# mLSTM v and o of two heads at a time by seven half-size products, attention output parked in DRAM, and another order of the heads' steps

## The chip, the cores and the metric

One core of a Trainium2 chip. Its engines work side by side, each through its own queue in order: PE (TensorE, matrix products, and transposes by an identity), ACT (ScalarE), DVE (VectorE), POOL (GpSimd, which here computes reciprocal square roots and issues DMAs, among them the ones that add to what lies in memory), SP (SyncE, which issues the plain weight loads). The metric is device time of one launch in microseconds, lower is better.

## The reference, cut to what matters

One layer of a decoder trunk: 512 tokens of width 1024, float32. A half-step feed-forward block, a mixer, a second half-step block, with RMS norms between. The mixer has a dilated attention and an mLSTM side by side:

```python
proj = h @ w_in     # attention q,k,v | mLSTM q,k (conv), v, o | mLSTM i,f | branch gates
...                 # attention: 3 groups of 4 heads of 128 channels, groups combined to att (512 x 512)
qk = jax.nn.silu(causal_depthwise_conv(qk_m, conv_w, conv_b))
q_m, k_m = jnp.split(qk, 2, axis=-1)              # mLSTM: 4 heads of 256 channels
hm = mlstm_chunkwise(q_m, k_m, v_m, ig, lf)       # heads are independent of each other
hm = hm * lax.rsqrt(jnp.mean(hm * hm, axis=-1, keepdims=True) + RMS_EPS)
hm = hm * head_g
ml = jax.nn.sigmoid(o_m) * hm
merged = jax.nn.sigmoid(g_a) * (att @ w_att_branch) + jax.nn.sigmoid(g_m) * (ml @ w_mlstm_branch)
return merged @ w_out
```

The change concerns `v_m` and `o_m`: the 512 x 1024 matrix h times 512 columns for each head (256 of v, 256 of o).

## The kernel before

Every float32 factor is held as two fp32r parts, high (`wh`, `hTh`) and low (`wl`, `hTl`); a product is three matmuls (high x high, low x high, high x low). `load_w` lets SP load a block of weights (512 KB) into `wf`, ACT cast it to `wh`, and DVE subtract to `wl`; `split` does the last two for a block that is in memory already.

Some products are done by seven half-size products instead of eight (Strassen's scheme in Winograd's form): tokens, inner dimension and columns are halved, and sums and differences of the quarters are multiplied. The token side's sums are made once (`token_sums`: parts 4, 5, 6, 7 in `x7`; the quarters themselves are 1, 2, 3) and partly parked in DRAM (`kept`), from where `reload6` and `reload4` fetch them. The weight side's sums are made by POOL's DMAs that add one block of DRAM to a tile: `v12_sums` and `v12_seven` for the attention's v of groups 1 and 2 (tiles `sum_x` and `sum_z`, products `pwa`, `pwb`, `pwc`). In `unit` DVE makes them, for the branch gates of the mLSTM (`gm1` to `gm7`).

Order of the mixer: q, k, scores, softmax and values of four attention head slots (`scores`, `turn`, `values`; the output of slot h goes to `atth[:, h]` and `attl[:, h]`, which stay in memory until the output branches). Then, for each of the four mLSTM heads: `m_vo` (v and o by plain products: four banks `pvo`, 96 matmuls of 128x512), `m_scores` (`pa`), a projection of the next head's q (`m_qk_proj`, tiles `pm`, 48 matmuls), `m_out` (`po`, then the normalisation: `dn`, ACT's squares `jm`, `vv`, POOL's `r_m`, `rr`, and the scaling of `so`), the next head's k projection, `m_decay` (`pb`, `gd`, `E`) and `m_turn` (transposes `pml` of `so` on PE). `m_qk_conv` is the convolution of q or k: two scalings `z` on ACT, six shifted adds on DVE, the tanh `th`, a product on DVE, cast `mqkh` and low part `mqkl`. In head 3 gate products take the place of the next head's projections. At the end come, for each of 8 column blocks, the gates and the two branches `p2[0]` (attention) and `p2[1]` (mLSTM).

The order within each engine's queue is settled when the kernel is built: a scheduler orders the instructions from the order of the code and their dependences, and `issue_after` holds one back behind a named other. At run time each queue is worked off in that order, so an instruction that waits holds up all behind it.

Of the kernel before, what the change touches and what calls it, by code (L numbers as in the profile page):

```python
# [39 lines left out]
def tile_hybrid_block(ctx: ExitStack, tc: tile.TileContext, a: dict):  # L40
# [759 lines left out]
    for k in "57":  # L800
        parts_at[k] = ap_.tile([P, 8, H], F32R, tag="v12", bufs=2, name=f"part{k}")
# [84 lines left out]
    sum_x, sum_z = (ap_.tile([P, 2, D], F32, tag=tag, bufs=1, name=f"sum_{tag}") for tag in ("sm", "pT"))  # L886

    def v12_block(k, g):
        return a["wv12"][{"g": 0, "u": 1}[k[0]], 2 * int(k[1]) + g]

    def v12_load(out, k, g, add=False):
        if add:
            nc.gpsimd.dma_start(out[:, g, :], v12_block(k, g), accum_op=ADD)
        else:
            nc.gpsimd.dma_start(out[:, g, :], v12_block(k, g))
# [12 lines left out]
    def v12_seven():
        steps = [(k, g) for k in "1562734" for g in range(2)]
        direct = {"1": "g0", "2": "g1", "4": "u1"}  # L910
        w = {}

        def prep(n):
            if n >= len(steps):
                return
            k, g = steps[n]
            if k in direct:
                w[k, g] = load_w(v12_block(direct[k], g), f"w12{k}{g}")
                return
# [12 lines left out]
        pa, pb, pc = (pair(f"pw{x}") for x in "abc")
        out = {"1": pa, "2": pa, "5": pc, "3": pc, "6": pb, "7": pb, "4": pb}
        flat = [[const.tile([P, 2, 512], F32, tag=f"x{x}", bufs=1, name=f"v12flat_{hp}{x}") for x in xx]
                for hp, xx in enumerate(((3, 1), (2, 0)))]
        for n, (k, g) in enumerate(steps):
            prep(n + 3)
            (xh, xl), (wh, wl) = x7[k], w.pop((k, g))
# [7 lines left out]
            if not g:  # L946
                continue
            for i in range(2):
                q1, o = flat[1][0][:, i, :], out[k][i]
                late = flat[1 if k in "57" else 0][1][:, i, :]  # L950
                if k == "1":
                    nc.scalar.copy(q1, o)
                elif k in "56":
                    nc.vector.tensor_tensor(late, o, q1, op=ADD)
                elif k == "2":
                    nc.scalar.copy(flat[0][0][:, i, :], o)
                elif k == "7":
# [19 lines left out]
        return vs  # L977
# [81 lines left out]
    def values(h, pT, v12):  # L1059
# [11 lines left out]
        nc.vector.tensor_tensor(attl[:, h, :], o, atth[:, h, :].bitcast(F32), op=ALU.subtract)  # L1071

# [47 lines left out]
    def token_sums():  # L1120
# [44 lines left out]

    summed = []
# [483 lines left out]
```

## Time and profile before

| | |
|---|---|
| runs | 2645.49, 3396.49 and 1324.98 us, median 2645.49 |
| profiled execution | 1325.25 us, span of the core 1323.5 us, mean granted clock 0.998 |
| busy share | PE 99%, PE weight loads 90%, DVE 77%, ACT 49%, POOL 8% |
| attention's v by seven products | about 400 to 440 us from the span's start |
| mLSTM heads | about 601 to 809 us |
| branches and gates behind them | to about 990 us |

The profiled execution agrees with the lowest of the three runs; the median is about twice as long. Times inside the profile are microseconds from the start of the span. A row of the timeline has start, length, engine, line, operation, output<-inputs, and in brackets the idle time ahead of it with what ended it. Groups of instructions have busy time, mean ns of one, and idle time ahead.

### The profile page before, as it was taken

How to read it: one execution, taken by the hardware profiler on the slowest of the kernel's cores; microseconds unless marked ns; L12 is line 12 of the kernel's file. 1: busy time of each engine (PE TensorE's matmuls, PEld its weight loads, DVE VectorE, ACT ScalarE, POOL GpSimd, SP SyncE). 2: the span in 40 equal slices, each digit the busy share in tenths (PEclk: the TensorE clock that was granted, in tenths of full speed). 3: DMA queues.
4: the chain of work that ended last, by engine and by line, in shares of the span. 5: the costliest groups of instructions: out<-in, count | busy, mean ns of one | idle time of the engine just before them, and what ended most of it. 6: DMA issues, size and time to landing. Idle time of an engine off the chain costs nothing.

```text
span 1323.5 us, 20795 instructions
## 1 busy us (share of the span) xinstructions
PE 1315.3 (99%) x8237; PEld 1189.2 (90%) x8237; DVE 1015.8 (77%) x1569; ACT 646.4 (49%) x1049; POOL 102.2 (8%) x152
## 2 busy tenths in 40 slices
PE   9999999999999999999999999999999999999997
PEld 9999999888998888888888889999889999999886
DVE  7999898888885666775756755766379999897887
ACT  6444444565644443644535444443265444445663
POOL 1000000230421100000000000000010000001220
PEclk9999999999999999999999999999999999999999
DMA  5233332796498832222222223335413333335991
GB/s 199 94 107 107 103 111 96 199 241 160 157 296 233 283 115 96 80 80 74 70 85 78 77 81 111 101 108 187 147 42 100 108 103 107 102 111 146 268 175 64
DMA packets 48881, 172.15 MB, mean 130 GB/s; under 512 B 5476, under 2 KB 6508, under 8 KB 48528
## 3 DMA queue, kind: packets, MB, share of 16 engines
q1 hardware_dynamic: 32544, 115.13, 25.7%
q0 software_dynamic: 16224, 55.70, 16.7%
q8 instruction: 64, 1.05, 0.3%
q14 instruction: 33, 0.27, 0.1%
q10 hardware_dynamic: 16, 0.00, 0.0%
HBM read 160.33 MB, written 10.49 MB: 129 GB/s over the span
## 4 chain that ended last, share of the span: by engine, by line
PE 99%; DVE 1%; POOL 0%; issue 0%; ACT 0%; DVEq 0%; POOLq 0%; ACTq 0%
PE qb_b L338 10%; PE qb_a L338 10%; PE pq L189 8%; PE pm L189 7%; PE p L189 6%; PE qa_a L338 4%; PE qa_b L338 4%; PE qb_gm L1198 4%; PE acc_o L243 3%; PE accb_b L537 3%; PE accb_a L537 3%; PE pvo L1326 2%; PE pvo L1328 2%; PE pvo L1327 2%; PE accc_b L537 2%; PE accc_a L537 2%
## 5 line engine op out<-in xcount | busy, mean ns | idle before, releaser
L189 PE MATMUL pq<-hTh_mx,wh_qk 128*128 128x512 f32 x160 | 63.2, 395 | 0.0
L189 PE MATMUL pq<-hTl_mx,wh_qk 128*128 128x512 f32 x160 | 62.4, 390 | 0.0
L189 PE MATMUL pm<-hTh_mx,wh_mqk 128*128 128x512 f32 x128 | 50.3, 393 | 0.0
L1326 PE MATMUL pvo<-wh_vo,hTh_mx 128*128 128x512 f32 x128 | 50.2, 392 | 0.0
L99 DVE TENSOR_TENSOR wl_qk<-wf_qk,wh_qk 128x1024 fp32r<-128x1024 f32 x24 | 29.3, 1223 | 26.9 <-PE pq L189 18.9
L189 PE MATMUL pm<-hTl_mx,wh_mqk 128*128 128x512 f32 x128 | 49.9, 390 | 0.0
L1328 PE MATMUL pvo<-wl_vo,hTh_mx 128*128 128x512 f32 x128 | 49.9, 390 | 0.0
L1327 PE MATMUL pvo<-wh_vo,hTl_mx 128*128 128x512 f32 x128 | 49.8, 389 | 0.0
L99 DVE TENSOR_TENSOR wl_mqk<-wf_mqk,wh_mqk 128x1024 fp32r<-128x1024 f32 x16 | 19.6, 1225 | 31.9 <-ACT wh_mqk L85 22.2
L85 ACT CAST wh_qk<-wf_qk 128x1024 fp32r<-128x1024 f32 x24 | 25.0, 1047 | 33.1 <-PE pq L189 12.1
L263 ACT CAST wh_a<-cd_a 128x1024 fp32r<-128x1024 f32 x19 | 19.9, 1049 | 40.8 <-DVE cd_a L263 40.8
L263 ACT CAST wh_b<-cd_b 128x1024 fp32r<-128x1024 f32 x19 | 19.9, 1049 | 40.5 <-DVE cd_b L263 40.5
L189 PE MATMUL pq<-hTh_mx,wl_qk 128*128 128x512 f32 x160 | 39.6, 389 | 0.0
L338 PE MATMUL qa_a<-hTh_f,wh_a 128*128 128x256 f32 x152 | 38.2, 284 | 0.0
L338 PE MATMUL qa_b<-hTh_f,wh_b 128*128 128x256 f32 x152 | 38.2, 284 | 0.0
L338 PE MATMUL qa_a<-hTl_f,wh_a 128*128 128x256 f32 x152 | 38.1, 283 | 0.0
L338 PE MATMUL qa_b<-hTl_f,wh_b 128*128 128x256 f32 x152 | 38.1, 283 | 0.0
L1091 DVE SCALAR_TENSOR_TENSOR z<-pm,cw,z 128x511 f32<-128x511 f32 (+2 forms) x48 | 35.3, 744 | 1.4 <-ACT z L1089 0.9
L189 PEld LDWEIGHTS pq<-hTh_mx,wl_qk 128*128 128x128 f32 x160 | 30.0, 188 | 6.2
L189 PEld LDWEIGHTS pq<-hTh_mx,wh_qk 128*128 128x128 f32 x160 | 30.1, 188 | 6.1
L189 PEld LDWEIGHTS pq<-hTl_mx,wh_qk 128*128 128x128 f32 x160 | 30.1, 188 | 6.0
L85 ACT CAST wh_mqk<-wf_mqk 128x1024 fp32r<-128x1024 f32 x16 | 16.8, 1048 | 37.2 <-PE pvo L1327 22.9
(722 smaller groups left out, 4556.5 us busy)
## 6 DMA issues: line engine op xcount, KB each, us to landing
wf_qk<-in_wqk SPq DMA_DIRECT2D x24, 512.0 KB, 4.1
g_a<-in_wgu SPq DMA_DIRECT2D x19, 512.0 KB, 3.7
u_a<-in_wgu SPq DMA_DIRECT2D x19, 512.0 KB, 3.7
g_b<-in_wgu SPq DMA_DIRECT2D x19, 512.0 KB, 3.7
u_b<-in_wgu SPq DMA_DIRECT2D x19, 512.0 KB, 3.7
wf_mqk<-in_wmqk SPq DMA_DIRECT2D x16, 512.0 KB, 3.3
wf_vo<-in_wvo SPq DMA_DIRECT2D x16, 512.0 KB, 3.2
T_a<-in_wdq POOLq DMA_DIRECT2D x12, 512.0 KB, 10.3
```

The lines of the kernel that those rows point to most:

```text
L85: return nc.scalar.copy(wh, wf)
L99: nc.vector.tensor_tensor(wl[:, :m], wf[:, :m], wh[:, :m].bitcast(F32), op=ALU.subtract)
L189: nc.tensor.matmul(out, lhsT=wt[:, k * P:(k + 1) * P], rhs=x[:, k, 0:T], start=n == 0, stop=n == len(terms) - 1)
L243: nc.tensor.matmul(out, lhsT=x[:, tk], rhs=w[:, cs], start=first and n == 0, stop=last and n == 2, skip_group_check=True)
L263: self.last[eng] = getattr(getattr(nc, eng), fn)(*args, **kw).ins
L338: nc.tensor.matmul(out, lhsT=wt[:, i * P:(i + 1) * P], rhs=y[:, i, :], start=first and n == 0, stop=last and n == len(terms) - 1, skip_gro ...
L537: nc.tensor.matmul(o, lhsT=x[:, tk], rhs=w[:, cs], start=k in "1256" and g + m + n == 0, stop=False, skip_group_check=True)
L1091: nc.vector.scalar_tensor_tensor(z[:, s:], src[:, :T - s], cw[:, ct, 3 - s:4 - s], z[:, s:], op0=ALU.mult, op1=ALU.add)
L1198: nc.tensor.matmul(out, lhsT=wt[:, i * P:(i + 1) * P], rhs=y[:, i, :], start=first and m == 0, stop=last and m == len(terms) - 1, skip_gro ...
L1326: nc.tensor.matmul(out, lhsT=hTh[:, k, tk], rhs=wh[:, cs], start=k == 0, stop=False)
L1327: nc.tensor.matmul(out, lhsT=hTl[:, k, tk], rhs=wh[:, cs], start=False, stop=False)
L1328: nc.tensor.matmul(out, lhsT=hTh[:, k, tk], rhs=wl[:, cs], start=False, stop=k == KD - 1)
```

## The change

1. The seven products of `v12_seven` become a generator `wide_seven` that serves other weights too. Its order is 1, 1, 5, 5, 2, 6, 6, 2, 7, 7, 3, 3, 4, 4 (digit: product; the second digit in `WIDE`: which half of the inner dimension). Its sums go into one tile of two halves, to which POOL's DMAs add in three rounds (`u0`, plus `u1` for product 5; plus `g0` for 6; plus `g1` for 3); product 7 has a weight block of its own. The writes of parts 4 to 7 to DRAM come behind the last addition.
2. `m_vo` goes. `vo_pair(p)` computes v and o of heads 2p and 2p+1 by `wide_seven`, head 2p as the first 512 columns and head 2p+1 as the second: 7 x 2 x 12 = 168 matmuls of 128x512 for two heads instead of 192. Head 2p's results go straight to `vm` and `so`; head 2p+1's are left in two float32 tiles, from which `raw_v` and `raw_o` take them later. DVE and ACT combine the products in `evac`.
3. Each slot's attention output is written to DRAM (`att_kept`) as soon as it is there; parts 6 and 4 are loaded into its memory for the products of both pairs, and it is fetched back behind pair 1.
4. The heads' steps are in another order, written out by hand: pair 0, with the convolutions of head 0 and the decay of head 0 between its products; heads 0 and 1; pair 1, with head 1's transpose between; heads 2 and 3. Behind head 3, the first attention branch stands ahead of head 3's transpose. The hold on head 3's normalisation (`issue_after(summed[0].ins)`) goes. Two pools get `reuse_waits="tile"`.

```diff
+    WIDE = "10 11 50 51 20 60 61 21 70 71 30 31 40 41".split()
+    FROM = {"1": "g0", "2": "g1", "4": "u1"}
+
+    def wide_sums(block, sums, after=None):
         for g in range(2):
+            with tc.issue_after(after) if after else nullcontext():
+                nc.gpsimd.dma_start(sums[g], block("u0", g))
+        for g in range(2):
+            nc.gpsimd.dma_start(sums[g], block("u1", g), accum_op=ADD)
+
+    def wide_seven(block, sums, name, evac, added=None):
...
+        def fetch(n):
+            if n < len(WIDE) and WIDE[n][0] == "7":
...
+                nc.sync.dma_start(f7[g], block("g0", g))
+                nc.gpsimd.dma_start(f7[g], block("u0", g), accum_op=ADD)
 
         def prep(n):
...
+            split(f7[g] if k == "7" else sums[g], *w[n])
+            if k in "56":
+                i = nc.gpsimd.dma_start(sums[g], block({"5": "g0", "6": "g1"}[k], g), accum_op=ADD)
...
+            fetch(n + 5)
             prep(n + 3)
...
@@ values(h, ...)
         nc.scalar.copy(atth[:, h, :], o)
         nc.vector.tensor_tensor(attl[:, h, :], o, atth[:, h, :].bitcast(F32), op=ALU.subtract)
+        for d, t in zip(att_kept, (atth, attl)):
+            nc.gpsimd.dma_start(d[h], t[:, h, :])
...
+    def vo_block(p):
+        return lambda k, g: a["wvo"][2 * p + "gu".index(k[0]), 2 * int(k[1]) + g]
+
+    def vo_pair(p, sums):
...
+        def evac(k, out):
...
+                if k == "1":
+                    nc.scalar.copy(q1[:, i, :], o)
+                elif k == "5":
+                    plus(late1[:, i, :], o, q1[:, i, :])
+                elif k == "6":
+                    plus(late0[:, i, :], o, q1[:, i, :])
+                elif k == "7":
+                    minus(f[:, i, :], o, late1[:, i, :])
+                elif k == "4":
+                    minus(f[:, i, :], o, q1[:, i, :])
+                else:
+                    j, v = (i, o) if k == "2" else (2 + i, late0[:, i, :])
+                    if k == "3":
+                        plus(v, o, v)
+                    take_v(vm, j, v)
+                    take_o(h, so, j, v)
...
-            with tc.issue_after(summed[0].ins):
-                end()
...
+    vo = vo_pair(0, vo_sums(0))
+    for k, tag in (("6", "attl"), ("4", "atth")):
...
+            nc.gpsimd.dma_start(flatten(v), d)
+    qk = new_mqk(0)
+    steps(vo, 1)
+    for pi in range(2):
+        m_qk_conv(0, pi, pqs[pi], qk)
+    steps(vo, 12)
     E = m_decay(0)
+    steps(vo, 3)
+    EE = m_scores(0, qk, E)
...
+    EE = m_scores(3, qk, E)
+    reload4()
+    late = branch_gates(1)
+    next(late)
+    m_out(3, EE, vms[3], sos[3])
...
+    p2 = att_branch(0)
+    m_turn(3, sos[3])
```

Three places show how the queues move. A number behind a name tells instances apart.

First, ACT's queue behind the cast of the attention's last output. `mqkh0` and `z01` belong to the convolutions of head 0's q and k, `E0` to its decay. Before:

```order
L1070 CAST atth_4939<-o3_6188 128x512
L1096 CAST mqkh0_6213<-z00_6215 128x1024
L1354 ACTIVATE E0_6248<-gd0_6246,cT_4983 128x128
L1357 ACTIVATE E0_6248<-pb0_6243,cT_4983 128x384
L1354 ACTIVATE E0_6248<-gd0_6246,cT_4983 128x128
L1357 ACTIVATE E0_6248<-pb0_6243,cT_4983 128x256
L1354 ACTIVATE E0_6248<-gd0_6246,cT_4983 128x128
L1089 ACTIVATE z01_6229<-pm01_0_6102,cw_3988 128x512
L1089 ACTIVATE z01_6229<-pm01_1_6103,cw_3988 128x512
L1357 ACTIVATE E0_6248<-pb0_6243,cT_4983 128x128
L1354 ACTIVATE E0_6248<-gd0_6246,cT_4983 128x128
```

After, with `vo_Eh0` the copies of product 1, `th01` the tanh of k's convolution, and `wh_vo050`, `wh_vo051` the casts of the weight sums for the two halves of product 5 (`vo_x0h` and `vo_x0l` are the tiles of the sums):

```order
L1087 CAST atth_a_4936<-o3_6193 128x512
L1322 ACTIVATE vmh0_6229<-ident_79 128x4x2
L1323 ACTIVATE vml0_6230<-ident_79 128x4x2
L1115 CAST mqkh0_6240<-z00_6259 128x1024
L1108 ACTIVATE z01_6273<-pm01_0_6107,cw_3988 128x512
L1108 ACTIVATE z01_6273<-pm01_1_6108,cw_3988 128x512
L1362 COPY vo_Eh0_6226<-vo0p1_0_6287 128x512
L1362 COPY vo_Eh0_6226<-vo0p1_1_6288 128x512
L1112 ACTIVATE th01_6274<-z01_6273 128x1024
L254 CAST wh_vo050_6254<-vo_x0h_6220 128x1024
L1115 CAST mqkh0_6240<-z01_6273 128x1024
L254 CAST wh_vo051_6289<-vo_x0l_6221 128x1024
```

The decay of head 0 is gone from here, and the casts of product 5's weights stand behind the copies of product 1 and behind `th01`.

Second, POOL's queue at the end of the attention. Before, nothing but the last loads for the attention, the load of `hg` (the gains of the heads) and the first reciprocal roots of the mLSTM:

```order
L971 DMA v12_1_4929<-v12rows_1_4924 128x2048
L976 DMA part70_4935<-kept7h_4015 128x1024
L1294 DMA hg_5630<-in_mlstm_head_g 128x1024
L114 TENSOR_TENSOR r_m00_6541<-vv00_6539,nhalf_84 128x2
L114 TENSOR_TENSOR r_m01_6583<-vv01_6581,nhalf_84 128x2
```

After, from the weight blocks of product 7 on. L892 are plain loads of `u0`, L894 additions of `u1`, L904 additions to product 7's blocks, L1505 the reloads of parts 6 and 4; the two `att_kept` rows are those of the last slot:

```order
L904 DMA wf_vo070_6345<-in_wvo 128x1024
L904 DMA wf_vo071_6367<-in_wvo 128x1024
L892 DMA vo_x0h_6220<-in_wvo 128x1024
L1090 DMA att_kepth_4938<-atth_a_4936 128x512
L1090 DMA att_keptl_4939<-attl_a_4937 128x512
L892 DMA vo_x0l_6221<-in_wvo 128x1024
L894 DMA vo_x0h_6220<-in_wvo 128x1024
L1505 DMA part6_m_6234<-kept6h_4012 128x1024
L894 DMA vo_x0l_6221<-in_wvo 128x1024
L1505 DMA part6_m_6234<-kept6l_4013 128x1024
L1505 DMA part4_m_6237<-kept4h_4008 128x1024
L1505 DMA part4_m_6237<-kept4l_4009 128x1024
```

The writes of the last slot and part 6's reload are mixed with the loads and additions for product 5.

Third, DVE's queue at the normalisation of head 3. `t1_1` with `qb_gm1` is a result of gate unit `gm1`, `u_gm2`, `g_gm2` and `wl7_gm2` prepare the weights of unit `gm2`. Before:

```order
L1403 TENSOR_SCALAR vv30_7844<-ssm30_7825 128x2
L1408 TENSOR_TENSOR rr30_7848<-r_m30_7846,dn30_7824 128x2
L1411 SCALAR_TENSOR_TENSOR so3_7696<-po30_0_7822,rr30_7848,so3_7696 128x256
L1411 SCALAR_TENSOR_TENSOR so3_7696<-po30_1_7823,rr30_7848,so3_7696 128x256
L1395 TENSOR_TENSOR dn31_7854<-po31_1_7853,cT_4983 128x1
L1396 SCALAR_TENSOR_TENSOR dn31_7854<-po31_1_7853,dn31_7854 128x1
L1397 RECIPROCAL dn31_7854<-dn31_7854 128x2
L1403 TENSOR_SCALAR vv31_7886<-ssm31_7855 128x2
L1182 TENSOR_TENSOR t1_1_7892<-qb_gm1_7919,q1_gm1_7893 128x2x256
L1408 TENSOR_TENSOR rr31_7984<-r_m31_7888,dn31_7854 128x2
L1411 SCALAR_TENSOR_TENSOR so3_7696<-po31_0_7852,rr31_7984,so3_7696 128x256
L1411 SCALAR_TENSOR_TENSOR so3_7696<-po31_1_7853,rr31_7984,so3_7696 128x256
```

After:

```order
L1594 SCALAR_TENSOR_TENSOR t1_0_7790<-t1_0_7790,p2_0_0_8071 128x512
L1186 TENSOR_TENSOR u_gm2_8167<-g_gm2_8166,u_gm2_8167 128x512
L1186 TENSOR_TENSOR t1_1_7895<-qb_gm1_7922,q1_gm1_7896 128x256
L1186 TENSOR_TENSOR g_gm2_8166<-g_gm2_8166,u_gm2_8167 128x512
L1186 TENSOR_TENSOR g_gm2_8166<-g_gm2_8166 128x512
L255 TENSOR_TENSOR wl7_gm2_8183<-u_gm2_8167,wh7_gm2_8182 128x1024
L1450 TENSOR_SCALAR vv30_8009<-ssm30_7990 128x2
L1455 TENSOR_TENSOR rr30_8013<-r_m30_8011,dn30_7989 128x2
L1458 SCALAR_TENSOR_TENSOR so3_7777<-po30_0_7987,rr30_8013,so3_7777 128x256
L1458 SCALAR_TENSOR_TENSOR so3_7777<-po30_1_7988,rr30_8013,so3_7777 128x256
L1450 TENSOR_SCALAR vv31_8051<-ssm31_8020 128x2
L1455 TENSOR_TENSOR rr31_8055<-r_m31_8053,dn31_8019 128x2
```

`vv30`, `rr30` and the first scaling of `so3`, which stood ahead of a result of `gm1`, now follow its last result (`t1_1<-qb_gm1,q1_gm1`, which reads the product that PE runs directly ahead of the transposes `pml3`) and three preparations for `gm2`.

More of the change, by code (lines that the diff above doesn't have):

```diff
@@ L930, in v12_seven @@
         for n in range(3):
             prep(n)
[L932 to L936, printed above, removed]
+        yield
+        out = {}
+        for n, (k, g) in enumerate(WIDE):
+            g = int(g)
+            if k in "156" and not g:
+                p = pair(f"{name}p{k}")
+                out.update({x: p for x in {"1": "12", "5": "53", "6": "674"}[k]})
+            fetch(n + 5)
@@ L1472, in tile_hybrid_block, with steps @@
-    for _ in late:
-        pass
+    def steps(gen, n):
+        for _ in range(n):
+            next(gen, None)
+    vo = vo_pair(0, vo_sums(0))
+    for k, tag in (("6", "attl"), ("4", "atth")):
+        t = low.tile([P, 8, H], F32R, tag=tag, bufs=1, name=f"part{k}_m")
+        x7[k] = [halves_of(t, i) for i in range(2)]
+        for v, d in zip(x7[k], kept[k]):
+            nc.gpsimd.dma_start(flatten(v), d)
[3 more added lines that the diff above has]
+        m_qk_conv(0, pi, pqs[pi], qk)
@@ new lines, in tile_hybrid_block @@
+    vo = vo_pair(1, sums)
+    steps(vo, 5)
+    m_turn(1, sos[1])
+    steps(vo, 8)
+    E = m_decay(2)
+    steps(vo, 3)
+    atth, attl = new_att("m")
+    for d, t in zip(att_kept, (atth, attl)):
+        nc.gpsimd.dma_start(t, d.rearrange("h p t -> p h t"))
+    EE = m_scores(2, qk, E)
+    qk = new_mqk(3)
+    m_qk_conv(3, 0, m_qk_proj(3, 0), qk)
+    m_out(2, EE, vms[2], sos[2])
+    m_qk_conv(3, 1, m_qk_proj(3, 1), qk)
+    E = m_decay(3)
+    raw_v(3)
+    m_turn(2, sos[2])
+    raw_o(3)
@@ new lines, in tile_hybrid_block, with load_branch, att_branch @@
+    reload6()
+    next(branch_gates(0, False))
+    EE = m_scores(3, qk, E)
[3 more added lines that the diff above has]
+    m_out(3, EE, vms[3], sos[3])
+    def load_branch(dt):
+        if dt % 2 == 0:
+            branch[0] = load_w(a["wA"][dt // 2], f"wA{dt}")
+        branch[1] = load_w(a["wM"][dt], f"wM{dt}")
+    def att_branch(dt):
+        load_branch(dt)
+        p2 = pair(f"p2_{dt}")
+        o = (dt % 2) * 512
+        ws(p2[0], [w[:, o:o + 512] for w in branch[0]], HEADS, atth, attl, (late, 6))
+        for _ in late:
+            pass
+        return p2
@@ L1489, in tile_hybrid_block @@
     mlTh, mlTl = Tiles(0), Tiles(1)
[L1490 removed]
     for dt in range(KD):
[L1492 to L1500 removed]
+        p2 = p2 if dt == 0 else att_branch(dt)
+        ws(p2[1], branch[1], KD, mlTh, mlTl)
         t1 = t1s[dt]
```

258 lines of the change are left out of this document (118 added, 140 removed).

## The prediction

> **What bounds the kernel now.** I read the shares of busy time first, then the chain that ended last, and then the timeline of TensorE where the change sits. The first fence is the page of the kernel before: the span, the line on busy time, PE's busy tenths and its granted clock in 40 slices, the chain by engine (followed back from the last instruction, with the share of the span each engine holds) and one of the three groups of products that the change replaces.
>
> ```profile
> span 1323.5 us, 20795 instructions
> PE 1315.3 (99%) x8237; PEld 1189.2 (90%) x8237; DVE 1015.8 (77%) x1569; ACT 646.4 (49%) x1049; POOL 102.2 (8%) x152
> PE   9999999999999999999999999999999999999997
> PEclk9999999999999999999999999999999999999999
> PE 99%; DVE 1%; POOL 0%; issue 0%; ACT 0%; DVEq 0%; POOLq 0%; ACTq 0%
> L1326 PE MATMUL pvo<-wh_vo,hTh_mx 128*128 128x512 f32 x128 | 50.2, 392 | 0.0
> ```
>
> TensorE (PE) carries 99% of the chain, and its products of v and o never wait. So the time is the sum of what PE issues plus every moment in which PE has nothing to issue, and a new wait of PE costs its full length. The 392 ns are latency, not price: matmuls overlap. The price is the distance between starts, read from PE's timeline at the first product of head 1's v and o and at the first score product behind its 96.
>
> ```profile
> 655.09 0.47 PE L1326 MATMUL pvo<-wh_vo,hTh_mx 128*128 128x512 f32 x1
> 676.98 0.39 PE L1368 MATMUL pa<-mqkh 128*128 128x512 f32 x1
> ```
>
> (676.98 - 655.09) / 96 = **0.228 us** for one 128x512 matmul.
>
> **What is taken away.** Before, four heads take 4 x 96 = 384 such matmuls. After, two pairs take 7 products x 2 weight blocks x 12 = 168 each, 336 in all. 48 fewer x 0.228 = **-10.9 us**, all of it on PE. The additions that replace them go to DVE, ACT and DMAs. DVE is busy for 77% of the span on average, which alone says nothing about the moments at which PE waits, so those are worked out below.
>
> A second gain lies in the attention's v product, now in the order 1, 5, 2, 6. PE's timeline there, before:
>
> ```profile
> 427.35 0.61 PE L943 MATMUL pwa<-wl_w,hTh_mx 128*128 128x512 f32 x2
> 428.07 1.47 PE L943 MATMUL pwb<-wh_w,part 128*128 128x512 f32 x4
> ```
>
> The two matmuls start at 427.35 and 427.58, so the next could at 427.81, but product 7 starts at 428.07: 0.26 us. The four behind it spread over 1.47 - 0.39 = 1.08 us instead of 3 x 0.228, another 0.4, which may be a missing record. In the new order other products stand between the request of a sum and its use, so the wait goes: **-0.3 us**, bounds 0 (it stays) and -0.7.
>
> **The first pair's second product waits.** In the changed order, the pair of heads 0 and 1 starts right behind the attention. The rows from PE, ACT and DVE of before show what lies there:
>
> ```profile
> 601.74 0.49 PE L1347 MATMUL pb<-selr 4*128 4x512 f32 x1
> 601.85 0.59 ACT L1070 CAST atth<-o 128x512 fp32r<-128x512 f32 x1 [4.12 <-PE o L1068]
> 602.33 1.05 ACT L1096 CAST mqkh<-z 128x1024 fp32r<-128x1024 f32 x1
> 604.99 1.45 ACT L1089 ACTIVATE z<-pm,cw 128x512 f32<-128x512 f32 x2
> 609.94 1.06 ACT L1093 ACTIVATE th<-z 128x1024 f32<-128x1024 f32 x1 [0.94 <-DVE z L1091]
> 603.11 0.68 DVE L1071 TENSOR_TENSOR attl<-o,atth 128x512 fp32r<-128x512 f32 x1
> 603.70 1.22 DVE L1097 TENSOR_TENSOR mqkl<-z,mqkh 128x1024 fp32r<-128x1024 f32 x1
> 605.80 4.04 DVE L1091 SCALAR_TENSOR_TENSOR z<-pm,cw,z 128x511 f32<-128x511 f32 x6 [0.89 <-ACT z L1089]
> 611.03 1.23 DVE L1094 SCALAR_TENSOR_TENSOR z<-th,z 128x1024 f32<-128x1024 f32 x1
> L85 ACT CAST wh_mqk<-wf_mqk 128x1024 fp32r<-128x1024 f32 x16 | 16.8, 1048 | 37.2 <-PE pvo L1327 22.9
> L99 DVE TENSOR_TENSOR wl_mqk<-wf_mqk,wh_mqk 128x1024 fp32r<-128x1024 f32 x16 | 19.6, 1225 | 31.9 <-ACT wh_mqk L85 22.2
> ```
>
> Before, this chain (cast, low part, two scalings, six shifted adds, tanh `th` at 609.94) ran beside 96 matmuls and delayed nothing. After, ACT's queue has the cast of weight sum 50 (`wh_vo050`) **behind** that `th` (front matter, first place). `th` cannot be much earlier: its scalings wait for `mqkl` (603.70 + 1.22 = 604.92), the six adds for the scalings, and the chain starts from the same cast of the attention's last output. PE frees at 601.74 and has products 10 and 11: 24 x 0.228 = 5.5 us, to 607.2. The cast can start at 609.94 + 1.06 = 611.0, ends at 612.05, and product 50 starts at 612.1. That is **4.9 us of waiting whatever the sums do**, so it is the floor of this term.
>
> The sum itself may be later. Rows for the queue of GpSimd (POOL): two issues, then the times from issue to landing of the two tiles of v sums (plain and accumulating transfers mixed; first `sum_sm`, then `sum_pT`).
>
> ```profile
> 404.99 0.53 POOL L895 DMA_DIRECT2D sum_sm<-in_wv  x1 [14.12 <-DVE wl_w L255]
> 409.49 0.90 POOL L893 DMA_DIRECT2D sum_sm<-in_wv  x1 [3.97 <-DMA sum_sm<-in_wv]
> DMA to landing us min/median/max: 4.2/7.3/11.9
> DMA to landing us min/median/max: 7.3/9.3/13.9
> ```
>
> The plain load issued at 404.99 is the shortest, 4.2 us: the next issue waits for it until 409.49. Accumulations are the long ones. In the changed queue (second place) the two writes of the last attention head, waiting for ACT's and DVE's casts, stand ahead of everything that pair 0 still needs. `attl` starts on DVE when `atth` is done (602.45) and ends at about 603.2; its write issues until 603.8, the plain load of the second sum until 604.4, and the first accumulation into `vo_x0h` goes out at 604.4. With the median of 7.3 us it lands at 611.7. The cast then ends at 612.75, and product 50 starts at 612.8: **5.6 us** instead of 4.9.
>
> The rest of the pair, with the same prices (cast 1.05, low part 1.22, landing 7.3; the low part is needed 0.9 us after its product starts, so each late sum adds some 0.3 us):
> - 51: `vo_x0l`'s load (issued 603.8) lands at 608.1, its accumulation is issued then and lands at 615.4, is cast by 616.5, and is needed at 612.8 + 2.75 + 0.3 = 615.9: 0.7, with the low parts of 50 and 51 1.3 us.
> - 60: the next accumulation into `vo_x0h` goes out after 50's low part (614.0), lands at 621.3, is cast by 622.4, and is needed behind 51 and 20 at about 622.3: 0.1, with the low part 0.4 us.
> - 61: out at 617.8, landed at 625.1, cast at 626.2, needed at 625.4: 0.8, with the low part 1.1 us.
> - 21, 70, 71, 30, 31, 40, 41: their weights are there; 30's last accumulation has 13 us between 60's split and its use.
>
> The sum is 5.6 + 1.3 + 0.4 + 1.1 = **8.4 us**; bounds 5.0 (only `th` binds; landings of 4.2 us) and 22 (landings of 13.9 us, worked out under the rivals). I take the median of `sum_sm`, the nearest row: the same size, kind and queue.
>
> The second pair issues its sums during head 1, over 20 us before their use: nothing. Its rsqrt of head 1 stands on POOL behind two accumulations that wait for splits done by then: nothing. The attention's reload and the writes of heads 0 to 2 lie under 100 us of other work: nothing. Scores of head 1 now come 12.3 us behind the last product of its k (one convolution, one `pb`, one transpose and 48 matmuls), against the 10.5 us that the same chain took before; some 1 us of added ACT and DVE work eats most of the slack: 0, bounds 0 and 1.5.
>
> **The last transpose waits.** Before, head 3's normalisation ran on DVE ahead of the next unit's weights; after, it stands behind them (third place). Rows of before: PE at the transposes, DVE and POOL in the normalisation, and the groups of the operations that are now ahead.
>
> ```profile
> 807.30 0.65 PE L1198 MATMUL qb_gm<-part,wl_gm 128*128 128x256 f32 x4
> 807.79 1.03 PE L1424 MATMUL pml<-ident,so 128*128 128x128 f32 x8
> 800.34 0.17 DVE L1403 TENSOR_SCALAR vv<-ssm 128x2 f32<-128x2 f32 x1 [0.59 <-ACT jm L1400]
> 801.40 0.16 DVE L1408 TENSOR_TENSOR rr<-r_m,dn 128x2 f32<-128x2 f32 x1 [0.90 <-POOL r_m L114]
> 805.18 0.69 DVE L1182 TENSOR_TENSOR t<-qb_gm,q_gm 128x512 f32<-128x512 f32 x1 [0.77 <-PE qb_gm L1198]
> 805.98 0.88 DVE L1411 SCALAR_TENSOR_TENSOR so<-po,rr,so 128x256 f32<-128x256 f32 x2
> L1182 DVE TENSOR_TENSOR t<-qb_gm,q_gm 128x256 f32<-128x256 f32 x7 | 2.9, 419 | 0.4 <-PE qb_gm L1198 0.4
> L1182 DVE TENSOR_TENSOR g_gm<-g_gm,u_gm 128x512 f32<-128x512 f32 x7 | 4.8, 682 | 0.0
> L1182 DVE TENSOR_TENSOR g_gm<-g_gm 128x512 f32<-128x512 f32 x7 | 4.8, 690 | 0.2
> L255 DVE TENSOR_TENSOR wl_gm<-u_gm,wh_gm 128x1024 fp32r<-128x1024 f32 x7 | 8.5, 1220 | 0.5 <-ACT wh_gm L254 0.5
> ```
>
> Before, the transposes start at 807.79, right where the row above them says, and `so` is ready at 806.86. After, DVE's `t` reads the last product of the very unit that PE runs directly ahead of the transposes. So from the end S of that product: 0.3 us until DVE sees it, then 0.42 + 0.68 + 0.69 + 1.22 = 3.0, then `vv` to `rr` over POOL 801.40 - 800.34 = 1.06, `rr` 0.2 and the first `so` 0.48: the first transpose can start at S + 5.0, where before it started without a wait. Its second `so` adds 0.2. The second half then takes 0.4 for that `so`, 1.06 + 0.2 + 0.48 and a last 0.2, against 0.67 us of PE work in between: 1.7. The term is 5.0 + 0.2 + 1.7 = **6.9 us**; bounds 5 (DVE's neighbours overlap) and 9.
>
> **The sum.** The profiled execution took 1325.25 us around its span of 1323.5. The median of the three runs shown, 2645.49, is about twice that and the lowest, 1324.98, agrees with it; I forecast the execution that the profile shows. 1325.25 - 10.9 - 0.3 + 8.4 + 6.9 = **1329 us**, 0.3% slower. About 2% (26.5 us: below 1298.7 or above 1351.8) is what a measurement of this kernel can tell from no change.
>
> **Rivals.**
> - *One of the two waits is hidden* (1321, 15%). If the sums land as the plain load did and only `th` binds, some 6 us are left in the pair; if one of the two places doesn't wait at all, 1325.25 - 11.2 + 6.9 = 1321. For it: POOL is busy for 8% only, and the queues' orders leave it open how far DVE runs ahead. Against: neither `th` at 609.94 nor DVE's place behind PE's last product depends on the sums. Without any wait the time would be 1314, still within 2%.
> - *PE's clock falls in the new gaps* (1333, 25%). At the start the trace has a slow stretch: the first 17 small matmuls take 3.81 us, later 8 take 1.04.
>
> ```profile
> 1.06 3.81 PE L74 MATMUL warm<-warm 128*128 128x256 bf16 x17 [1.06 <-DVE nhalf L81]
> 6.20 1.04 PE L74 MATMUL warm<-warm 128*128 128x256 bf16 x8
> ```
>
>   That is 0.22 against some 0.11 us between starts, on a PE that had been idle (the slices' clock doesn't show it). Afterwards no slice of 33 us is busy for under nine tenths but the last, so the trace has no gap of 5 us from which to tell whether one brings the slow stretch back. If each of the two gaps does, half of 3.8 us is lost twice: 1329 + 3.8 = 1333. The Trainium skill, TensorE: Matmul & The Clock Gate, Part 1 (The HAM clock gate), says that after one idle window of about 3.4 us, counted by a free-running clock, PE runs at half rate until a busy window has passed. By that rule, which speaks against this change, a gap of 5 us holds a whole window about every other time, and one of the two gaps would cost some 1.7 us, an estimate from that page: 1331. The start of the trace agrees with the rule.
> - *Accumulations land late* (1343, 10%; the other side). At 13.9 us each, 50 starts at 604.4 + 13.9 + 1.1 = 619.4 (12.2 late), 60 waits a further 6.7, 51, 61 and 30 about 1.4 each: 23 + 6.9 - 11.2 gives 1344. It decides from where the first pair's waits exceed 11.2 - 6.9 = 4.3 us, which already `th` does; above 2% it would need landings of some 17 us, longer than any of these rows.
> - *The change doesn't do what it says*: the 48 matmuls are absent from PE's order, so this has no chance worth a number.
>
> **Chances and range.** Forecast 50% (1324 to 1334), small waits 15%, clock 25%, late sums 10%. Range 1318 to 1340, leaving out most of the late sums and a gain without waits. Faster by over 2% 0.02, within 0.95, slower 0.03.
>
> **What would show it.** 336 products of v and o at 0.228 us; on PE a gap of 5 to 6 us ahead of product 50, released by ACT's cast, that cast starting behind `th`; smaller gaps at 51 and 61; a gap of about 5 us ahead of `pml` of head 3, released by `so`; matmul starts further apart than 0.228 us only behind these gaps, if at all. I am wrong if product 50 starts within 2 us of 11's end, if DVE runs `vv` of head 3 early, or if PE waits at scores or transposes of heads 0 to 2.

## The result, and the profile after

| | before | after |
|---|---|---|
| time, median | 1325.0 us | 1338.7 us (1337.1 to 1339.1) |
| ratio, 95% interval | | 1.0101 [1.0088, 1.0114] |
| profiled execution, span | 1325.25, 1323.5 us | 1337.08, 1335.1 us |
| PE instructions | 8237 | 8189 |

The kernel before, and run 2 below, also have executions of 2.0 to 2.6 times the time (2645, 3396 and 3016 us), and every comparison here leaves those out. The change made the kernel 1.0% slower; 0.3% was forecast. (The interval is 0.13% wide to each side, so far less than the 2% that the prediction names can be told from no change.) The page of the kernel after: span, busy time, PE's busy tenths and its granted clock in 40 slices, and the chain by engine.

```profile
span 1335.1 us, 20826 instructions
PE 1311.5 (98%) x8189; PEld 1182.4 (89%) x8189; DVE 1040.9 (78%) x1601; ACT 657.7 (49%) x1065; POOL 122.7 (9%) x180
PE   9999999999999999997999998999999999999997
PEclk9999999999999999998999998999999999999999
PE 89%; DVE 4%; issue 3%; DMA 3%; POOL 1%; ACT 1%; POOLq 0%; DVEq 0%; ACTq 0%
```

48 matmuls fewer, and PE's share of the chain falls from 99% to 89%. Two slices that were full are no longer: the one from 601 us (the first pair) and the one from 801 us (the last transposes). In both the clock falls too.

PE's timeline of the first pair after; columns as before, and in brackets PE's idle time and what ended it:

```profile
606.89 0.61 PE L936 MATMUL vo0p<-wl_vo,hTh_mx 128*128 128x512 f32 x2
613.08 2.08 PE L936 MATMUL vo0p<-wh_vo,part 128*128 128x512 f32 x4 [5.57 <-ACT wh_vo L254]
615.80 1.91 PE L936 MATMUL vo0p<-wh_vo,part 128*128 128x512 f32 x4
617.51 0.96 PE L936 MATMUL vo0p<-wl_vo,part 128*128 128x512 f32 x2
618.31 1.10 PE L936 MATMUL vo0p<-wh_vo,part 128*128 128x512 f32 x4
625.05 1.20 PE L936 MATMUL vo0p<-wh_vo,part_m 128*128 128x512 f32 x4 [1.03 <-ACT wh_vo L254]
629.56 1.20 PE L936 MATMUL vo0p<-wh_vo,part_m 128*128 128x512 f32 x4 [1.15 <-ACT wh_vo L254]
636.01 1.52 PE L936 MATMUL vo0p<-wh_vo,part 128*128 128x512 f32 x4 [0.36 <-issue]
```

Product 50 starts 5.57 us late, as forecast. But look at the rows behind it: the 12 matmuls of 50 take from 613.08 to 618.31, 0.436 us each instead of 0.228. The windows of the same trace (stretch, length, PE busy, weight loads, DVE, ACT, POOL, then PE's granted clock, DMA share and GB/s) say why:

```profile
607.20:613.00 5.80, 0.31 (x2) 0.00 (x0) 3.97 (x6) 3.15 (x5) 2.25 (x4) 0.86 1.04 268
613.00:618.30 5.30, 5.22 (x12) 4.14 (x13) 3.30 (x3) 2.96 (x4) 1.13 (x2) 0.51 1.04 280
618.40:620.50 2.10, 2.10 (x11) 1.69 (x10) 1.32 (x2) 0.00 (x0) 0.87 (x1) 1.00 0.98 248
822.10:826.20 4.10, 3.61 (x12) 2.80 (x13) 1.97 (x6) 1.08 (x2) 0.69 (x1) 0.50 0.18 73
```

The clock is granted at 0.51 for five microseconds behind the gap and at 1.00 from 618.4 (it falls inside the gap already, which is why the first row shows 0.86); behind the second large gap it is 0.50. The 40 slices of the page hide this: a slice of 33 us shows it as an 8.

ACT and POOL beside it, after:

```profile
610.04 1.06 ACT L1112 ACTIVATE th<-z 128x1024 f32<-128x1024 f32 x1 [1.65 <-DVE z L1110]
611.98 1.04 ACT L254 CAST wh_vo<-vo_x0h 128x1024 fp32r<-128x1024 f32 x1 [0.88 <-DMA vo_x0h<-in_wvo]
616.28 1.04 ACT L254 CAST wh_vo<-vo_x0l 128x1024 fp32r<-128x1024 f32 x1 [2.31 <-DMA vo_x0l<-in_wvo]
623.95 1.04 ACT L254 CAST wh_vo<-vo_x0h 128x1024 fp32r<-128x1024 f32 x1 [5.68 <-DMA vo_x0h<-in_wvo]
604.73 0.93 POOL L894 DMA_DIRECT2D vo_x0h<-in_wvo  x1
611.31 0.89 POOL L1505 DMA_DIRECT2D part_m<-kept6l  x1
612.36 0.90 POOL L1505 DMA_DIRECT2D part_m<-kept4l  x1
614.58 0.87 POOL L916 DMA_DIRECT2D vo_x0h<-in_wvo  x1 [1.32 <-DVE wl_vo L255]
```

The first addition, issued at 604.73, is cast at 611.98: 7.2 us, where 7.3 was assumed. The next one into the same tile, issued at 614.58 right behind the reloads of parts 6 and 4, is cast at 623.95: **9.4 us**.

The last transposes after, on PE, DVE and ACT:

```profile
816.77 0.64 PE L1202 MATMUL qb_gm<-hTh_mx,wl_gm 128*128 128x256 f32 x4
822.18 1.09 PE L1469 MATMUL pml<-ident,so 128*128 128x128 f32 x4 [4.77 <-DVE so L1458]
824.10 1.11 PE L1469 MATMUL pml<-ident,so 128*128 128x128 f32 x4 [0.41 <-DVE so L1458]
817.50 0.42 DVE L1186 TENSOR_TENSOR t<-qb_gm,q_gm 128x256 f32<-128x256 f32 x1
820.29 0.16 DVE L1450 TENSOR_SCALAR vv<-ssm 128x2 f32<-128x2 f32 x1
821.55 0.88 DVE L1458 SCALAR_TENSOR_TENSOR so<-po,rr,so 128x256 f32<-128x256 f32 x2
818.62 0.47 ACT L1447 ACTIVATE jm<-po,dn 128x256 f32<-128x256 f32 x1
```

The order is as forecast, DVE's `t` at 817.50 and `so` only at 821.55. But ACT's squares `jm` (the last row), which `vv` needs, also run only at 818.62, behind `t`. The prediction didn't look at that.

Two waits were not forecast. In the attention, PE waits for a weight's low part (`wl_qk`) on DVE, which a token sum (`tokens`, in the new order) now runs ahead of; at head 1's transpose, a low part of the second pair's weights stands ahead of `so`:

```profile
348.43 1.22 DVE L1125 TENSOR_TENSOR tokens<-hTh_mx,hTl_mx 128x1024 f32<-128x1024 f32 x1
354.47 1.21 PE L203 MATMUL pq<-hTh_mx,wl_qk 128*128 128x256 f32 x8 [0.88 <-DVE wl_qk L99]
724.54 1.23 DVE L255 TENSOR_TENSOR wl_vo<-vo_x1h,wh_vo 128x1024 fp32r<-128x1024 f32 x1
726.21 0.83 PE L1469 MATMUL pml<-ident,so 128*128 128x128 f32 x4 [0.38 <-DVE so L1458]
```

For the account below I took the distance between the starts of neighbouring matmuls and subtracted what the first of the two takes back to back (0.227 us for 512 columns, 0.120 for 256, 0.110 for 128). What is left over, in us, by stretch of the span, for both kernels and for every run:

| | 340-392 | 392-445 | 600-660 | 660-720 | 720-790 | 790-840 |
|---|---|---|---|---|---|---|
| before | -0.1 | 0.4 | 0.8 | 0.3 | 0.3 | 0.1 |
| after | 1.0 | -0.3 | 13.4 | 0.4 | 2.0 | 7.3 |

Over the whole span it is 29.2 after and 7.3 before: 21.9 more, less 10.9 for the absent matmuls, leaves 11.0 of the 11.6 us by which the span grew.

### The profile page after: what moved, and what is told of

Its sections match the earlier page's. It is cut to its first block, busy times and chain, and to the rows that moved or that the text cites. A ratio compares the mean times of both kernels' runs of the same rounds, so it can differ in the third digit from the quotient of the medians.

```text
span 1335.1 us, 20826 instructions
## 1 busy us (share of the span) xinstructions
PE 1311.5 (98%) x8189; PEld 1182.4 (89%) x8189; DVE 1040.9 (78%) x1601; ACT 657.7 (49%) x1065; POOL 122.7 (9%) x180
## 4 chain that ended last, share of the span: by engine, by line
PE 89%; DVE 4%; issue 3%; DMA 3%; POOL 1%; ACT 1%; POOLq 0%; DVEq 0%; ACTq 0%
PE qb_a L338 10%; PE qb_b L338 10%; PE pq L189 8%; PE p L189 6%; PE qa_a L338 4%; PE qa_b L338 4%; PE qb_gm L1202 4%; PE acc_o L243 3%; PE accb_b L537 3%; PE pm L189 3%; PE w12p L936 3%; PE accb_a L537 3%; PE vo1p L936 2%; PE accc_b L537 2%; PE accc_a L537 2%
## 5 line engine op out<-in xcount | busy, mean ns | idle before, releaser
L263 DVE TENSOR_TENSOR wl_a<-ab_a,wh_a 128x1024 fp32r<-128x1024 f32 x19 | 23.3, 1225 | 14.7 <-ACT wh_a L263 14.7
L263 DVE TENSOR_TENSOR wl_b<-ab_b,wh_b 128x1024 fp32r<-128x1024 f32 x19 | 23.3, 1225 | 14.7 <-ACT wh_b L263 14.7
L263 POOL DMA_DIRECT2D T_a<-in_wdq x12 | 11.1, 1181 | 238.3 <-DVE xl_a L263 228.9
L263 POOL DMA_DIRECT2D T_b<-in_wdq x12 | 10.8, 1157 | 236.2 <-PE acca_b L537 225.4
L189 PE MATMUL pm<-hTh_mx,wl_mqk 128*128 128x512 f32 x128 | 31.6, 389 | 0.0
```

What stands on the lines that cost most here:

```text
L189: nc.tensor.matmul(out, lhsT=wt[:, k * P:(k + 1) * P], rhs=x[:, k, 0:T], start=n == 0, stop=n == len(terms) - 1)
L263: self.last[eng] = getattr(getattr(nc, eng), fn)(*args, **kw).ins
```

## The experiments

Each is the changed kernel with one edit, unless it says otherwise; each median has its ratio to the kernel before, with the interval. `issue_after(x)` holds an instruction back behind x on its engine.

**1. The sums of product 5 first.** The writes of the last attention output move behind the additions of `u1`.

```diff
-        wide_sums(vo_block(p), sums)
+        last = wide_sums(vo_block(p), sums)      # returns its last addition
+        if p == 0:
+            with tc.issue_after(last):
+                keep_att(3)                      # the two att_kept writes of slot 3
```

> The loads and first additions of pair 0's sums go out ahead of the last slot's writes to DRAM (about 586 us instead of 604 us); with the sums early, the cast of 50 also comes out ahead of the tanh of k's convolution in ACT's queue. Theory (the first pair is limited by its sums and by what stands ahead of its casts): product 50 starts near 609.5 instead of 613.1, the gap of 5.7 us falls to about 2.4 us, half 51 doesn't wait, half 61 still waits a few us behind the reloads; 12.7 us of extra waiting become about 5: 1331 us (1329 to 1334). Rival (the clock after the gap is what costs, the sums come in time anyway): no more than the 2.5 us of the slow stretch is won, 1336 us or more.

1334.69 us, 1.0076 [1.0063, 1.0090]; 10.2 us left in the first pair.

```profile
609.80 1.19 PE L937 MATMUL vo0p<-wh_vo,part 128*128 128x512 f32 x4 [1.88 <-ACT wh_vo L254]
623.11 0.73 PE L937 MATMUL vo0p<-wh_vo,part_m 128*128 128x512 f32 x2 [1.57 <-DMA part_m<-kept6l]
630.24 1.20 PE L937 MATMUL vo0p<-wh_vo,part_m 128*128 128x512 f32 x4 [2.32 <-ACT wh_vo L254]
```

The gap ahead of 50 falls from 5.57 to 1.88 us. In this run the cast of 50 also stands ahead of `th01` on ACT (608.69, `th` at 610.45), so both the sum and the cast's place in the queue moved; runs 2 and 3 take them apart. Only 4.0 us of time come of it: the wait moves on to the reload of part 6 and to 61, and the clock falls behind the shorter gap too (0.52 from 612.4 to 615.1).

**2. The casts first.** `th01` behind the casts of 50 and 51, the copies of product 1 behind the cast of 50; the sums stay late.

```diff
-        nc.scalar.activation(th, zz, AF.Tanh, scale=0.5)
+        with tc.issue_after(hold) if hold is not None else nullcontext():   # hold: cast of 51
+            nc.scalar.activation(th, zz, AF.Tanh, scale=0.5)
```

> ACT's queue alone: the casts of 50 and 51 stand ahead of the tanh of k's convolution, POOL's queue stays. Theory (the later of two, sum and tanh, decides; the sum landed at 611.96 and the tanh was over at 611.10): nothing is won, product 50 starts at 613 as before and the time stays within 1 us of 1338.7. Rival (the tanh ahead of the cast is the wait, as the prediction's floor has it): product 50 starts some us earlier and the time falls to 1335 or below.

1339.43 us, 1.0102 [1.0086, 1.0117]: nothing won. The cast has no tanh ahead of it and still waits 5.62 us for the transfer.

```profile
613.48 1.04 ACT L254 CAST wh_vo<-vo_x0h 128x1024 fp32r<-128x1024 f32 x1 [5.62 <-DMA vo_x0h<-in_wvo]
```

**3. The sums first, the casts behind the tanh.** Edit 1, and the cast of 50 held behind `th01` (`issue_after(th_of[0, 1])`). This isolates the floor that the prediction set by `th`.

> The sums early as in the first kernel, but the cast of 50 held behind the tanh. Theory: the tanh ends at 611.1, product 50 starts at 612.2, the gap is 4.9 us as the prediction's floor, and only the waits behind it shrink: about 6 us left of 12.7, 1332 us (1330 to 1335). Rival (only the sums count): the gap at 50 vanishes and the time is 1329 us or below.

1330.60 us, 1.0047 [1.0034, 1.0059]; 7.0 us left in the first pair.

```profile
612.01 2.05 PE L941 MATMUL vo0p<-wh_vo,part 128*128 128x512 f32 x4 [4.39 <-ACT wh_vo L254]
```

A gap of 4.4 us (the floor was given as 4.9), the slow matmuls behind it, and no other wait in the pair. With run 2 this shows that the later of the two, sum and tanh, sets the gap. The scheduler now put the reloads ahead of the additions for 60 and 61, and these landed in time. So **a version with a longer first gap than experiment 1 is 4 us faster**: what comes behind the gap costs more than the gap.

**4. The squares elsewhere.** The unused output of head 3's squares goes to other memory. In the changed kernel it shares its memory (tag `gd`) with `q1` of gate unit `gm1`, which DVE's `t` reads; so ACT's first square has to wait for `t`.

```diff
-                junk = lp.tile([P, MDH], F32, tag="gd", bufs=1, name=f"jm{h}{i}{b}")
+                junk = lp.tile([P, MDH], F32, tag="E" if h == 3 else "gd", bufs=1, name=f"jm{h}{i}{b}")
```

> Head 3's squares write their unused result to the memory of E instead of gd. In the changed kernel they share gd with q1 of gate unit gm1, whose last reader is the result that waits for the product ahead of the transposes. Theory (that shared memory is what holds head 3's normalisation): the 4.9 us gap ahead of the last transposes and the second one of 1 us go, at most 1.5 us stay: 1338.7 - 6 = 1332.5 us (1331 to 1334). Rival (the place in DVE's queue holds it, as the prediction has it, and the queue would stay as it is): 1338.7 us, unchanged.

1331.83 us, 1.0050 [1.0037, 1.0062]: 6.9 us won. Left over from 790 to 840 us: 1.9 instead of 7.3.

```profile
811.63 0.47 ACT L1447 ACTIVATE jm<-po,dn 128x256 f32<-128x256 f32 x1 [2.00 <-DVE dn L1443]
819.46 1.04 PE L1469 MATMUL pml<-ident,so 128*128 128x128 f32 x8
```

The squares run 7 us earlier, for `dn` alone, and the eight transposes follow the products of `gm1` with no idle time. Shown: DVE's order at this place was a result of the shared memory.

**5. Part 4's reload later.** It is issued behind the additions that make the sums of 60 and 61.

```diff
+    with tc.issue_after(add_of["vo0", "51"]):    # the addition of g0 behind the cast of 51
+        bring("4", "atth")                       # the two reloads of part 4
```

> POOL's queue alone: the two reloads of part 4 stand behind the additions for product 6 instead of ahead of them. Theory (the additions took 9.4 and 9.6 us because they stood behind four reloads of 512 KB): they take 5 to 7 us, product 60 and 61 wait 0 to 1 us each instead of 1.6 and 1.8, and the time falls by about 3 us to 1336 (1335 to 1337). Rival (an addition takes over 9 us in this place whatever stands ahead of it): 1338.7 us, unchanged.

1337.77 us, 1.0097 [1.0084, 1.0111], which by time alone can't be told from the changed kernel. The additions now land 5.6 and 6.6 us after issue instead of 9.4 and 9.6, and the waits at 60 and 61 nearly go. But product 70 starts later:

```profile
635.53 1.51 PE L939 MATMUL vo0p<-wh_vo,part 128*128 128x512 f32 x4 [2.31 <-issue]
633.61 1.23 DVE L255 TENSOR_TENSOR wl_vo<-vo_x0h,wh_vo 128x1024 fp32r<-128x1024 f32 x1 [1.22 <-ACT wh_vo L254]
634.75 1.28 DVE L947 TENSOR_TENSOR vo_E<-vo0p,vo_Eh 128x512 f32<-128x512 f32 x2
```

So 1.2 us less is left over in the pair where 3 were expected. The mechanism holds (two reloads fewer ahead, about 3 us sooner). The profile names no releaser for the wait at 70, but the rows of DVE point to one. Product 7 adds onto product 6's result in the same two banks (`"674"` in the kernel), which `vo_E` has to read first. That read stands on DVE behind a low part for product 30, which itself waits for a late sum. The first of its two adds ends at 635.43, and product 70 starts at 635.53; in the changed kernel the same two are at 635.90 and 636.01. In run 3 `vo_E` runs at 628.94 and nothing waits at 70.

**6. The gap filled.** 24 matmuls into a spare bank ahead of product 50, 5.45 us of PE work that is not needed.

```diff
+            if name == "vo0" and n == 2:
+                spare = bank("spare")
+                for _ in range(24):
+                    nc.tensor.matmul(spare, lhsT=hTh[:, 0, 0:P], rhs=hTh[:, 0, :], start=True, stop=True,
+                                     skip_group_check=True)
```

> 24 matmuls of 128x512 into a bank that nobody reads stand on PE between products 11 and 50 of pair 0 (5.5 us, the length of the gap), nothing else is changed. Rival (the slow stretch behind the gap costs its 2.5 us): 1336 us. Theory (the slow stretch costs nothing here, since halves 51, 60 and 61 wait for sums that are requested independently of PE): starts behind the gap are 0.228 us apart, the waits at 51 and 60 are longer by as much, and the time stays at 1338.5 us within 1 us.

1336.50 us, 1.0089 [1.0076, 1.0103], an interval that overlaps the changed kernel's; filler and what is left over in the pair are 11.5 us together instead of 13.4. (Its profiled execution, 1339.6, is 3 us above the median, with an extra wait of 1.63 us at 419.79 and slow matmuls behind it.)

```profile
611.19 5.60 PE L934 MATMUL spare<-hTh_mx 128*128 128x512 f32 x24
621.65 1.19 PE L941 MATMUL vo0p<-wh_vo,part 128*128 128x512 f32 x4 [1.35 <-ACT wh_vo L254]
```

And PE's window there (stretch, length, PE busy, granted clock, DMA share, GB/s):

```profile
617.00:622.00 5.00, 3.58 (x14) 1.00 1.08 291
```

With useless work in the gap the pair is 1.9 us shorter, because product 50 then runs at full rate. My theory expected no gain from it, the rival 2.5: the trace speaks for the rival, while the times alone don't settle it. Not all 2.5 us return, since 51 now waits 1.35 us for a sum that the slow matmuls had covered.

**7. The attention's v alone.** The kernel before, with only the new order of the attention's seven products, token sums and weight sums.

```diff
-        steps = [(k, g) for k in "1562734" for g in range(2)]
+    WIDE = "10 11 50 51 20 60 61 21 70 71 30 31 40 41".split()
...
-        whole(f[1], *x7["3"])
+                     lambda: whole(f[2], *x7["1"]),
```

> The kernel before with only the part of the change that concerns the attention's v (order, sums, token sums, later writes). Theory: the short wait of v is gone (-0.7 us) and the 1.0 us wait in the first q product at 354 us is added: 1325.2 us, within 0.7 us of before. Rival (the new order of v gains what was forecast and the wait at 354 us comes from another part): 1324.5 us or below.

1325.80 us, 1.0008 [0.9999, 1.0017]: no difference that these runs can tell. The wait ahead of product 7 goes (392 to 445 us: -0.3 instead of 0.4), and the one at 354 us comes (1.0 instead of -0.1).

**8. All of these together** (edits 1, 2, 4 and 5).

> The changed kernel with early sums, casts of 50 and 51 ahead of the copies of product 1 and of the tanh, part 4 behind the additions for product 6, and head 3's squares in other memory. Theory (these waits are the whole difference): about 1 to 2 us of the 12.7 stay in pair 0 and 1 of the 7.2 at the last transposes: 1338.7 - 17 = 1321 us (1317 to 1324), faster than before by some 4 us. Rival (the waits move elsewhere): 1327 us or more.

1327.78 us, 1.0022 [1.0013, 1.0031]: a miss, 7 us above the theory. The cast of 50 is in time, but its low part on DVE stands behind six adds, and part 6's reload behind the additions:

```profile
611.35 0.73 PE L943 MATMUL vo0p<-wl_vo,part 128*128 128x512 f32 x2 [2.41 <-DVE wl_vo L255]
622.59 0.73 PE L943 MATMUL vo0p<-wh_vo,part_m 128*128 128x512 f32 x2 [2.51 <-DMA part_m<-kept6l]
```

**9. Both casts of product 5 ahead of the attention's end.** In the runs with the sums first these land 1 to 4 us before the attention ends, while ACT and DVE sit idle. So the casts of 50 and 51 move ahead of the cast of the attention's last output, and the copies of product 1, `mqkh0` and `z01` behind them.

```diff
+    steps(vo, 1)                                  # prepares 10, 11, 50 and 51
+    with tc.issue_after(cast_of["vo0", "51"]):
+        values_out(3, o_last)                     # atth, attl and the att_kept writes of slot 3
```

> Changed kernel, but in the first pair the sums for both halves of product 5 are loaded and added ahead of the write of the last attention output, and both of their casts (wh_vo050, wh_vo051) stand on ScalarE ahead of the cast of that output, in time in which ScalarE has nothing to do; the convolution of head 0's k, the copies of product 1 and everything else there come behind. The additions for 60 and 61 so go out some 10 us earlier. Nothing is left out. My theory (the first pair's 13.4 us are nothing but sums and casts that stand late in the queues, with a stretch at half rate behind the longest gap): no gap above 1 us from 600 to 660 us, no half-rate stretch, excess there 0 to 2 us instead of 13.4, so 1338.7 - 12 = 1326.5 us. Rival (the queues only hand the wait on, as in the two versions before): waits at the low part of 50, at 60 or at the reloaded parts of 7 to 9 us, 1333 us.

1327.12 us, 1.0021 [1.0012, 1.0029]; 2.9 us left in the first pair instead of 13.4.

**10. Run 9 with the squares elsewhere.**

> The run before with the unused output of head 3's squares in other memory as well (as in the run on the squares). Nothing is left out. My theory: the two add up, 1326.5 - 5.4 = 1321 us, 0.3% faster than the kernel before, since 10.9 us of products are gone and some 6 us of small waits are left (1 at 354 us, 1 to 2 at head 1's transposes, 2 at the last). Rival (waits move again): 1327 us, no faster than before.

1320.30 us, **0.9971 [0.9961, 0.9981]**: faster than before by 0.3%, and the fastest version of all. The span is 1318.2 us. ACT and PE:

```profile
597.73 1.05 ACT L254 CAST wh_vo<-vo_x0h 128x1024 fp32r<-128x1024 f32 x1 [3.56 <-DMA vo_x0h<-in_wvo]
600.32 1.05 ACT L254 CAST wh_vo<-vo_x0l 128x1024 fp32r<-128x1024 f32 x1 [1.54 <-DMA vo_x0l<-in_wvo]
602.13 0.59 ACT L1099 CAST atth_a<-o 128x512 fp32r<-128x512 f32 x1 [0.77 <-PE o L1094]
607.40 1.10 PE L943 MATMUL vo0p<-wh_vo,part 128*128 128x512 f32 x4
617.23 0.70 PE L943 MATMUL vo0p<-wh_vo,part_m 128*128 128x512 f32 x2 [0.41 <-DMA part_m<-kept6h]
```

Product 50 follows 11 with no gap, and the cast of the attention's output, at 602.13, is only 0.3 us later than before (601.85 there). What is left over by stretch, in the same columns as above, over all runs in which the first pair or the last transposes were edited:

| run | 600-660 | 660-720 | 720-790 | 790-840 |
|---|---|---|---|---|
| 1 sums first | 10.2 | 0.5 | 1.7 | 7.3 |
| 2 casts first | 12.9 | 0.3 | 3.2 | 7.7 |
| 3 sums first, casts behind tanh | 7.0 | 0.7 | 1.0 | 7.7 |
| 4 squares elsewhere | 13.4 | 0.4 | 2.5 | 1.9 |
| 5 part 4 later | 12.2 | 0.4 | 1.8 | 7.1 |
| 6 gap filled (with the filler) | 11.5 | 0.3 | 1.6 | 8.3 |
| 8 all | 9.1 | 0.5 | 1.3 | 1.9 |
| 9 casts before the attention's end | 2.9 | 1.2 | 0.9 | 7.8 |
| 10 run 9, squares elsewhere | 1.5 | 1.7 | 1.0 | 1.9 |

## Why the prediction was wrong

The sign and both large waits were right; the size was not: +13.7 us of median where +3.75 was forecast, inside the range at its upper end. Term by term, from the profiled executions:

- **48 matmuls, -10.9**: right. They are absent, and run 10, in which most waits are gone, is 5.3 us of span faster than before with 5.0 us of waits more.
- **Product 50, 5.6 us**: right to 0.1 (5.7), and so was its cause: the addition landed after 7.2 us. That the size fits so well is luck: 7.3 was the median of 4.2 to 11.9 us, and the next addition into the same tile took 9.4. The floor by `th`, 4.9, was 4.4 in run 3.
- **PE's clock, 0**: the step that failed most. The prediction kept it as a rival at 25% with 3.8 us for both gaps, and its sum had none of it. Measured: 2.5 us in product 50 and 1.0 behind the last transposes, 3.5 together, close to the rival's 3.8. The Trainium skill, TensorE: Matmul & The Clock Gate, Part 1 (The HAM clock gate), gives 426.7 ns between starts of 512 columns at half rate; the 0.427 us here (615.80 to 617.51 for four) agrees. By that rule, as the prediction read it, each gap of 5 us had about an even chance. In the traces here the chance was far higher: all 12 gaps of over 4 us, in all runs, brought half rate.
- **51, 60 and 61, 2.8 us**: mis-sized, 0, 1.7 and 1.8, and 1.0 for product 70, to which nothing was given: 4.5 together. (By the prediction's own figures its 0.7 at 51 is 0.5.) The wait at 51 was covered by the slow matmuls. Those at 60 and 61 came from additions that took 9.4 and 9.6 us, not the median of 7.3: the prediction quoted the queue's order with the four reloads in it and gave them no price. Run 5 shows the price: two reloads fewer ahead, and they land after 5.6 and 6.6 us. Nor are accumulations as such "the long ones": in the trace before, four plain loads issued 0.5 us apart from 359.79 on landed after 6.8 to 9.0 us. At 70 the prediction looked at the weights alone ("their weights are there") and not at DVE's read of product 6's banks (run 5).
- **Last transposes, 6.9 us**: 7.2 measured, of which 1.0 is the clock. The size was right, the cause only half: DVE's place behind `t` comes from memory that ACT's squares share with an operand of `t` (run 4). The order of an engine's queue showed what happens; what forces it stood in the tiles' tags.
- **Attention's v, -0.3**: the wait did go (-0.7), but with a new one of 1.1 us at 354 us, which the prediction did not look for, though it named the token sums' new order as part of the change. Run 7: together nothing that can be told.
- **The second pair and heads 1 to 3, 0 with up to 1.5**: 1.7 us more from 720 to 790 us, of which 0.5 is the wait at 726 us, at head 1's transpose, one of the signs of being wrong that the prediction named. The rest was not traced.
- **The rival of late accumulations** (1343, all landings at 13.9 us) did not happen as told: the first ones were on time, only those behind the reloads were late.

In sum: 3.5 (clock) + 0.1 (50) + 1.7 (51 to 70: 4.5 instead of 2.8) + 1.1 (354 us) + 1.7 (720 to 790), less 0.7 (transposes without the clock) and 0.4 (attention's v), is 7.0 of the 8.1 us between the forecast and the profiled execution, 1337.1; the rest I can't place. The median lies another 1.6 above that.

## What to carry to other kernels

Where an engine is busy for 99% of the span, saving its work pays only if nothing new makes it wait: here 10.9 us of products went, and 22 us of waits and slow matmuls came, most of it behind instructions that stood late in ACT's, DVE's and POOL's queues. Look for idle time of those engines ahead of the place: moving two casts and five transfers 12 to 18 us forward (run 9) took away 10.5 us of waits, while three partial repairs mostly handed the wait on to the next in the queue. And when an order looks forced, look at which tiles share memory: an output that nobody reads held the tail for 5 to 7 us.

## What the runs showed of the hardware

Half rate came behind gaps shorter than those of the changed kernel. In run 6's trace one idle time of 1.63 us was enough, and in run 8's one of 2.41 us (611.35, above) brought none, while the next one there, 2.51 us ahead of 622.59, did. Over all traces, 12 of 12 gaps of over 4 us brought half rate, and 4 of 19 gaps between 1.0 and 2.6 us.

Below that it matters where a gap falls. The traces hold the moments at which the granted clock changes. In the changed kernel it is 0.50 from 611.41 to 618.23 and from 819.62 to 826.45 us; these four moments are 2, 59 and 2 times 3.413 us apart. In the other traces, too, the changes lie whole multiples of 3.413 us apart, and a stretch at half rate between the first and the last lasts one or two such lengths. Cut at these moments, PE's windows are (stretch, length, PE busy, granted clock, DMA share, GB/s), two of run 6 and then two of run 8:

```profile
417.00:420.40 3.40, 1.77 (x8) 1.00 0.66 114
420.42:423.80 3.38, 3.38 (x9) 0.50 0.48 80
606.66:610.07 3.41, 2.25 (x9) 1.00 0.00 0
610.07:613.48 3.41, 2.13 (x9) 1.00 0.03 7
```

Run 6's gap lies within one window, which is 1.77 us busy, and the next one runs at half rate. Run 8's longer gap is cut in two at 610.07, each window is over 2 us busy, and nothing happens. So no length of a single short gap decides in these runs. The Trainium skill, in the part named above, speaks of a free-running window of 3413 ns; the traces agree with that length. That a window of 1.77 us busy suffices means that it need not be wholly idle. Here the measurement goes further than the page. The limit lies near half a window; one of 1.55 us busy (run 2, from 607.27) brought no half rate, so busy time as the profile shows it doesn't give it more exactly.

The place also sets the cost: ahead of the last transposes the same gap of 4.77 us left 7.1 to 8.3 us over from run to run (last column of the table). The 8.3 is run 6's, where the half rate starts at 823.18 and the gap ends at 823.55, so that nearly all of it falls on work; in the changed kernel it starts at 819.62, 2.6 us ahead of the gap's end.
